# Split products that stream their moving operand, and write PSUM, from the last column to the first

## The chip, the cores and the metric

One core of one Trainium2 chip runs the whole program in one launch. The metric is the device time of that core in microseconds (us), from the median of several executions. The times of the engines come from one further execution that the hardware profiler recorded.

## The reference

512 tokens of width 1024 go through two blocks, all in float32. The first has two layers, each of them a half-weighted SwiGLU, a mixer (a bidirectional mLSTM in layer 0, a windowed attention in layer 1) and a second SwiGLU, with a layer norm after each. The second block has two layers of an HGRN2 mixer beside a sparse attention, and a SwiGLU, with RMS norms. Nearly all arithmetic lies in the projections `x @ w`:

```
def swiglu(x, w_in, w_out):
    gu = x @ w_in                      # 1024 -> 2 x 2816
    g, u = gu[..., :D_FF], gu[..., D_FF:]
    return (jax.nn.silu(g) * u) @ w_out
...
x = layer_norm(ALPHA * x + 0.5 * swiglu(x, ffn_w_in[l, 0], ffn_w_out[l, 0]), ...)   # six of these in all
...
p = x @ w_in                           # mLSTM, attention and the mixers of the second block
```

## The kernel before, in words

Activations lie with the features on the 128 partitions and the 512 tokens along the free axis, as eight tiles of 128x512. Every operand of a projection is split into two parts, a high part rounded to the type fp32r and the remainder (`split`, lines 171 to 177: ScalarE writes the high part, VectorE subtracts). A projection is then the sum of three products, high by high, high by low and low by high, accumulated in one PSUM bank. These are the split products. There are two places that issue them.

`mm3` (lines 202 to 208) takes a 128x128 block of the weights as the stationary operand and a token slice of the activations as the moving operand: all 512 tokens in `gemms` (kind "a") and in `out_head` and `out_early`, and a half of 256 tokens (HA, then HB) in `pre` and in `out_tail`. Its three products are lines 206, 207 and 208.

`gemms` (kind "b", lines 262 to 268) makes products whose result has tokens on the partitions. There a 128x128 block of the activations is stationary and the rows of the weights move, n = 512, 280 or 256 columns at a time. Its three products are lines 266, 267 and 268.

In both, each product has a weight load of its own. The order of the work on TensorE is written out by the program: generators are interleaved by estimated costs (`run`, `tick`), and each engine executes its instructions in that order. A semaphore makes a product wait for the split of its operands. Weights come by DMA from the SyncE queue, 512 KB at a time (line 183). Between two stages the norm of the last one is finished in two halves of 256 tokens, so that `pre` can start on the half HA while the half HB is still being normalised (lines 464 to 471 write x, xh and xl).

Other products on TensorE are not split products of these two places: plain float32 products (the mLSTM scores at line 687 and its values at line 716, line 1250 and more), transposes, and the attention scores at lines 880 and 1391. All the products' operands are contiguous along the free axis, except the moving operand of line 1250, which takes every second run of m columns, m = 1 to 64. Five small copies on VectorE read backwards: lines 619, 621, 643, 646 and 649 read rows 32 to 36 with a step of -1, right beside a forward twin (618, 620, 642, 645, 648).

Of the kernel before, what the change touches and what calls it, by code (L numbers as in the profile page):

```python
# [56 lines left out]
class Core:  # L57
# [128 lines left out]
    def weights(self, src, n=1024, at=None):  # L186
# [12 lines left out]
        self.v(n)  # L199
        return h, l  # L200

    def mm3(self, out, w, k, xh, xl, start, stop):
        mm = self.nc.tensor.matmul
        wh, wl = (a[k // 4][:, k % 4 * 128:k % 4 * 128 + 128] if isinstance(a, tuple) else a[:, k * 128:(k + 1) * 128]
                  for a in w)
        mm(out, wh, xh, start=start, stop=False)  # L206
        mm(out, wh, xl, start=False, stop=False)  # L207
        mm(out, wl, xh, start=False, stop=stop)  # L208
# [22 lines left out]
    def gemms(self, jobs):  # L231

        units = deque()
        for j in jobs:
            if j[0] == "a":
                units.append((j[1], 1024))
            else:
                units.extend((s, 2 * j[2]) for s in j[1])
        ready = deque()

        def nxt():
            while units and len(ready) < 2:
                ready.append(self.weights(*units.popleft()))
            return ready.popleft()
        for j in jobs:
            if j[0] == "a":
                w = nxt()
                p = self.bank()
                for k in range(KD):
                    self.mm3(p, w, k, self.xh[k], self.xl[k], k == 0, k == KD - 1)  # L250
                    yield 0.65
                j[2](p)
            else:
                n = j[2]
                if len(j) > 4:
                    yield j[4]
                ps = [self.bank() for _ in range(4)]
                mm = self.nc.tensor.matmul
                for kp in range(4):
                    h, l = nxt()  # L260
                    for i in range(2):
                        k = 2 * kp + i
                        wh, wl = h[:, i * n:(i + 1) * n], l[:, i * n:(i + 1) * n]
                        for t in range(4):
                            ts = slice(t * 128, (t + 1) * 128)
                            mm(ps[t][:, :n], self.xh[k][:, ts], wh, start=k == 0, stop=False)  # L266
                            mm(ps[t][:, :n], self.xh[k][:, ts], wl, start=False, stop=False)  # L267
                            mm(ps[t][:, :n], self.xl[k][:, ts], wh, start=False, stop=k == KD - 1)  # L268
                            yield 0.65 * n / 512
                j[3](ps)  # L270
# [1404 lines left out]
```

## Time and profile before

| | |
|---|---|
| time, median of 3 runs | 3350.8 us (3350.4 to 3352.97) |
| the profiled execution: its time, its span | 3350.13 us, 3348.3 us |
| TensorE busy (products) | 3305.9 us, 99% of the span, 18704 instructions |
| TensorE busy (weight loads, beside the products) | 2827.0 us, 84% |
| VectorE, ScalarE, GpSimd busy | 1686.3 us (50%), 1280.9 us (38%), 96.1 us (3%) |
| mean granted TensorE clock | 0.996 |
| moved by DMA | 304.04 MB, mean 91 GB/s |

The span is the time from the first to the last instruction; the profiled execution took 1.83 us more. A product's recorded duration is longer than its place in the queue: products are pipelined, so the rate is read from the distance between starts. "128*128 128x512" in a row is the stationary operand's shape and the result's partitions and columns.

### The profile page before, as it was taken

The numbers are of one execution on the slowest core, as the hardware profiler recorded it, in microseconds if no ns is written. First come the engines' busy times: TensorE is split into PE (matmuls) and PEld (weight loads), VectorE is DVE, ScalarE is ACT, GpSimd is POOL, SyncE is SP. The second block draws the span as 40 slices with busy tenths as digits, with TensorE's granted clock in tenths as the row PEclk, the third lists the DMA queues.
The fourth block names the chain that finished last, engine by engine and source line by source line (L and its number), as shares of the span: only waits on it lengthen the run. The fifth ranks groups of instructions, "written<-read, shape, count | busy, mean of one in ns | idle before, by whom it ended". The sixth has DMA issues, their size and how long they took to land.

```text
span 3348.3 us, 46248 instructions
## 1 busy us (share of the span) xinstructions
PE 3305.9 (99%) x18704; PEld 2827.0 (84%) x18704; DVE 1686.3 (50%) x3451; ACT 1280.9 (38%) x2231; POOL 96.1 (3%) x138
## 2 busy tenths in 40 slices
PE   8999999999999999999999989999999999999999
PEld 7888977988898888879888978788888988898888
DVE  4333756733354333787334667775333567853332
ACT  3322545522233222685222433563232335632221
POOL 0000011000000000110000000000000000000000
PEclk9999999999999999999999989999999999999999
DMA  4333322233332333212333523112333332023333
GB/s 143 96 94 97 100 76 64 89 97 98 93 109 89 100 94 108 74 41 89 95 98 98 163 88 94 45 51 82 99 95 94 107 115 64 26 72 102 98 101 95
DMA packets 88918, 304.04 MB, mean 91 GB/s; under 512 B 9857, under 2 KB 12417, under 8 KB 88705
## 3 DMA queue, kind: packets, MB, share of 16 engines
q1 hardware_dynamic: 88704, 301.10, 29.3%
q8 instruction: 146, 2.39, 0.3%
q14 instruction: 68, 0.55, 0.0%
HBM read 298.96 MB, written 2.10 MB: 90 GB/s over the span
## 4 chain that ended last, share of the span: by engine, by line
PE 94%; DVE 3%; ACT 2%; DMA 1%; issue 1%; POOL 0%; DVEq 0%; SPq 0%; ACTq 0%; POOLq 0%
PE b L206 26%; PE b L208 26%; PE b L207 26%; PE b L267 2%; PE b L268 2%; PE b L266 2%; PE b L1250 1%; PE b L1442 1%; PE b L1391 1%; PE b L1420 1%; PE b L716 1%; ACT wh L174 1%; DVE wl L177 1%; PE b L1303 1%; DMA wr<-w_in 1%
## 5 line engine op out<-in xcount | busy, mean ns | idle before, releaser
L174 ACT ACTIVATE wh<-wr 128x1024 fp32r<-128x1024 f32 (+3 forms) x532 | 545.0, 1026 | 1568.1 <-PE b L207 980.5
L177 DVE TENSOR_TENSOR wl<-wr,wh 128x1024 fp32r<-128x1024 f32 (+3 forms) x532 | 628.3, 1183 | 867.2 <-ACT wh L174 864.9
L206 PE MATMUL b<-xh,wh 128*128 128x512 f32 (+1 forms) x2712 | 1021.7, 378 | 9.5 <-ACT xh L174 7.4
L208 PE MATMUL b<-xh,wl 128*128 128x512 f32 (+1 forms) x2712 | 1008.8, 373 | 3.2 <-DVE wl L177 3.2
L207 PE MATMUL b<-xl,wh 128*128 128x512 f32 (+1 forms) x2712 | 1008.7, 373 | 2.9 <-DVE xl L177 1.8
L206 PEld LDWEIGHTS b<-xh,wh 128*128 128x128 f32 x2712 | 511.1, 189 | 105.5 <-issue 9.4
L208 PEld LDWEIGHTS b<-xh,wl 128*128 128x128 f32 x2712 | 512.5, 189 | 94.5 <-DVE wl L177 5.8
L207 PEld LDWEIGHTS b<-xl,wh 128*128 128x128 f32 x2712 | 513.1, 189 | 91.7 <-issue 3.5
L206 PE MATMUL b<-hh,wh 128*128 128x512 f32 (+1 forms) x1144 | 400.4, 350 | 0.0
L208 PE MATMUL b<-hh,wl 128*128 128x512 f32 (+1 forms) x1144 | 398.4, 348 | 0.0
L207 PE MATMUL b<-hl,wh 128*128 128x512 f32 (+1 forms) x1144 | 398.3, 348 | 0.0
L283 DVE SCALAR_TENSOR_TENSOR hf<-b,sg 128x512 f32<-128x512 f32 x132 | 90.7, 691 | 407.4 <-PE b L208 404.0
L206 PEld LDWEIGHTS b<-hh,wh 128*128 128x128 f32 x1144 | 216.5, 189 | 28.6 <-issue 1.0
L207 PEld LDWEIGHTS b<-hl,wh 128*128 128x128 f32 x1144 | 216.5, 189 | 28.5 <-issue 1.0
L208 PEld LDWEIGHTS b<-hh,wl 128*128 128x128 f32 x1144 | 216.5, 189 | 27.6
L267 PE MATMUL b<-wl,xh 128*128 128x512 f32 (+2 forms) x352 | 122.8, 349 | 4.3 <-DVE wl L177 4.2
L266 PE MATMUL b<-wh,xh 128*128 128x512 f32 (+2 forms) x352 | 125.1, 360 | 0.0
L268 PE MATMUL b<-wh,xl 128*128 128x512 f32 (+2 forms) x352 | 122.7, 349 | 0.0
L177 DVE TENSOR_TENSOR hl<-hf,hh 128x512 fp32r<-128x512 f32 x132 | 89.9, 685 | 0.0
L174 ACT ACTIVATE hh<-hf 128x512 fp32r<-128x512 f32 x132 | 82.8, 632 | 0.8
L1395 ACT ACTIVATE sc<-sc,nm 128x128 f32<-128x128 f32 (+3 forms) x128 | 71.1, 557 | 23.5 <-DVE nm L1393 22.5
L267 PEld LDWEIGHTS b<-wl,xh 128*128 128x128 f32 x352 | 67.2, 191 | 14.3 <-DVE wl L177 6.1
(408 smaller groups left out, 4122.1 us busy)
## 6 DMA issues: line engine op xcount, KB each, us to landing
wr<-w_in SPq DMA_DIRECT2D x176, 512.0 KB, 3.7
wr<-b_win SPq DMA_DIRECT2D x88, 512.0 KB, 3.7
wr<-w_out SPq DMA_DIRECT2D x80, 512.0 KB, 3.5
wr<-b_wout SPq DMA_DIRECT2D x36, 512.0 KB, 3.5
wr<-w_out SPq DMA_DIRECT2D x36, 384.0 KB, 3.1
wr<-b_out SPq DMA_DIRECT2D x20, 512.0 KB, 3.6
wr<-b_w SPq DMA_DIRECT2D x16, 512.0 KB, 3.8
wr<-b_wout SPq DMA_DIRECT2D x16, 384.0 KB, 3.2
```

Of the source, the lines that this page charges most:

```text
L174: nc.scalar.activation(h, src, AF.Copy)
L177: nc.vector.tensor_sub(l, src, h.bitcast(F32))
L206: mm(out, wh, xh, start=start, stop=False)
L207: mm(out, wh, xl, start=False, stop=False)
L208: mm(out, wl, xh, start=False, stop=stop)
L266: mm(ps[t][:, :n], self.xh[k][:, ts], wh, start=k == 0, stop=False)
L267: mm(ps[t][:, :n], self.xh[k][:, ts], wl, start=False, stop=False)
L268: mm(ps[t][:, :n], self.xl[k][:, ts], wh, start=False, stop=k == KD - 1)
L283: nc.vector.scalar_tensor_tensor(hf, pu, half, sg, op0=OP.mult, op1=OP.mult)
L716: nc.tensor.matmul(p[:, :257], w[:, (j - j0) * 128:(j - j0 + 1) * 128], v[s][:, h], start=s == ss[0], stop=s == ss[-1])
L1250: nc.tensor.matmul(p[:, i * 64:(i + 1) * 64], K[h][:, ts], q, start=True, stop=True)
L1395: nc.scalar.activation(sc[:, :N], sc[:, :N], AF.Exp, bias=nm[:, g:g + 1], scale=-1.0, accum_out=sm[:, g:g + 1])
```

## The change

A helper is added that reverses the free axis of the result and of the moving operand, and the two places that issue split products call it. The stationary operand is as before. As result and moving operand are reversed together, each result column ends up where it was.

```diff
+    def mm(self, out, w, x, start, stop):
+
+        self.nc.tensor.matmul(out[:, ::-1], w, x[:, ::-1], start=start, stop=stop)
+
     def mm3(self, out, w, k, xh, xl, start, stop):
-        mm = self.nc.tensor.matmul
+        mm = self.mm
...
                 ps = [self.bank() for _ in range(4)]
-                mm = self.nc.tensor.matmul
+                mm = self.mm
                 for kp in range(4):
```

The attention scores, the plain float32 products and the transposes call TensorE directly and stay as they are. No instruction is added, removed or moved, and no transfer changes.

## Rows read from the trace of the kernel before

**Rows 1.** The page's part 1: engine, busy us, share of the span, instructions.

```profile
PE 3305.9 (99%) x18704; PEld 2827.0 (84%) x18704; DVE 1686.3 (50%) x3451; ACT 1280.9 (38%) x2231; POOL 96.1 (3%) x138
```

**Rows 2.** The view of cores: span and mean granted clock.

```profile
core 0: 3348.3 us, clock 0.996
```

**Rows 3.** The page's part 4, the chain that ended last: by engine, by line.

```profile
PE 94%; DVE 3%; ACT 2%; DMA 1%; issue 1%; POOL 0%; DVEq 0%; SPq 0%; ACTq 0%; POOLq 0%
PE b L206 26%; PE b L208 26%; PE b L207 26%; PE b L267 2%; PE b L268 2%; PE b L266 2%; PE b L1250 1%; PE b L1442 1%; PE b L1391 1%; PE b L1420 1%; PE b L716 1%; ACT wh L174 1%; DVE wl L177 1%; PE b L1303 1%; DMA wr<-w_in 1%
```

**Rows 4.** PE waits: engine, line, what it waited for, us, times, longest.

```profile
PE b L206 <- ACT xh L174: 7.4, 2, 6.4
PE b L398 <- DVE lns L489: 6.2, 1, 6.2
PE b L267 <- DVE wl L177: 4.2, 2, 2.1
```

**Rows 5.** Groups by line and form, PE: count, busy us, mean ns, idle before.

```profile
L206 PE MATMUL b<-xh,wh 128*128 128x512 f32 x2248 | 891.6, 397 | 0.0
...
L206 PE MATMUL b<-hh,wh 128*128 128x512 f32 x704 | 273.9, 389 | 0.0
...
L266 PE MATMUL b<-wh,xh 128*128 128x512 f32 x192 | 75.8, 403 | 0.0
...
L266 PE MATMUL b<-wh,xh 128*128 128x256 f32 x96 | 28.9, 302 | 0.0
...
L266 PE MATMUL b<-wh,xh 128*128 128x280 f32 x64 | 20.3, 318 | 0.0
```

**Rows 6.** Line 206 by operand names: a mixed name, and the last of 16.

```profile
L206 PE MATMUL b<-q,wh x64: 277/283/682, 1493.2 to 1551.7; 128*128 128x256 f32 x48, 128*128 128x512 f32 x16
...
L206 PE MATMUL b<-xh,mh x16: 280/283/283, 378.8 to 402.1; 128*128 128x256 f32 x16
```

**Rows 7.** Timeline, 512 columns, first and last of 134: start, us, engine, line.

```profile
1199.63 0.39 PE L207 MATMUL b<-xl,wh 128*128 128x512 f32 x1
...
1229.78 0.39 PE L208 MATMUL b<-xh,wl 128*128 128x512 f32 x1
```

**Rows 8.** Timeline, 256 columns, first and last of 27: start, us, engine, line.

```profile
349.80 0.28 PE L208 MATMUL b<-hh,wl 128*128 128x256 f32 x1
...
352.92 0.28 PE L207 MATMUL b<-hl,xh 128*128 128x256 f32 x1
```

**Rows 9.** Timeline, plain float32 products (L687) between split products.

```profile
448.94 1.02 PE L687 MATMUL b<-qk,qk 128*128 128x512 f32 x2
449.40 0.80 PE L206 MATMUL b<-xh,wh 128*128 128x512 f32 x1
450.04 0.40 PE L207 MATMUL b<-xl,wh 128*128 128x512 f32 x1
```

**Rows 10.** Chain in order of time, plain float32 of 257 columns: start, us, count.

```profile
498.02 1.30 PE b L716 x6
```

**Rows 11.** Timeline of VectorE: forward copy and backward twin, 512 and 1280 elements.

```profile
404.25 0.41 DVE L618 COPY ig<-z 32x512 f32<-32x512 f32 x1
404.67 0.42 DVE L619 COPY ig<-z 4x512 f32<-4x512 f32 x1
...
419.52 0.81 DVE L642 COPY Un<-UU 32x1280 f32<-32x1280 f32 x1
420.34 0.82 DVE L643 COPY Un<-UU 4x1280 f32<-4x1280 f32 x1
```

**Rows 12.** Timeline, line 1250: runs of m=1 (first) and m=64 (last).

```profile
2040.74 1.00 PE L1250 MATMUL b<-Q,K 128*128 128x64 f32 x8
...
2077.76 1.00 PE L1250 MATMUL b<-Q,K 128*128 128x64 f32 x8
```

**Rows 13.** Groups by line and form, VectorE, norm between stages.

```profile
L465 DVE TENSOR_TENSOR x<-x,b 128x256 f32<-128x256 f32 x96 | 40.0, 416 | 0.9
```

## The prediction

> **What bounds the kernel now.** First the totals [rows 1]: TensorE's products are busy 99% of the span, VectorE 50%, ScalarE 38%. The clock was granted at 0.996 of full speed [rows 2], so TensorE sits at its upper level of 2.4 GHz nearly throughout. Then the chain that ended last [rows 3]: 94% of it is TensorE, and lines 206, 207 and 208 alone are 26% each. The waits confirm it [rows 4]: the longest sum that the products ever waited for is 7.4 us, and the whole idle time of TensorE is 3348.3 - 3305.9 = 42.4 us. The reader is to see that there is no other bound in this kernel. What a split product costs, the kernel costs, and nothing lies above it that could hide an added nanosecond.
>
> How many split products there are, and of what size: line 206 has 4,712 under 16 names. Of these 2,248 + 704 have 512 columns [rows 5], and 64 more stand in five mixed names (16 each for q, K and Qs, 8 each for qk and mh) [rows 6]: 3,016. The other 1,696 have 256 columns. Line 266 adds 192 of 512, 96 of 256 and 64 of 280 [rows 5]. Each stands for three products, so 3 x (3,016 + 192) = 9,624 of 512 columns, 3 x (1,696 + 96) = 5,376 of 256 and 3 x 64 = 192 of 280: 15,192 of the 18,704 products are touched.
>
> Their present price comes from the distance of starts, not from the recorded durations. Of 134 products of 512 columns in a row, first and last start 30.15 us apart [rows 7]: 30.15 / 133 = 226.7 ns each. Of 27 with 256 columns they start 3.12 us apart [rows 8]: 3.12 / 26 = 120 ns. The difference, 106.7 ns for 256 columns, is 0.417 ns a column, one column in each cycle of 2.4 GHz. What is left, 226.7 - 213.4 = 13.3 ns, belongs to the product and not to its columns; for 280 columns that makes 130 ns. So split products take 9,624 x 0.2267 + 5,376 x 0.120 + 192 x 0.130 = 2,182 + 645 + 25 = 2,852 us, 85% of the span.
>
> **The change part by part.** No instruction comes, goes or moves; queues, waits, weight loads and DMAs are the same. Each of 15,192 products gets a step of -1 in two places. The moving operand is read from SBUF downwards, and the result is written to PSUM downwards and, in all but the first of each accumulation, added to what is there. So the whole change is: 15,192 times (the price of a column read downwards and written downwards, less 0.417 ns, times the columns, plus whatever a downward start costs).
>
> The trace of before has no product with a negative step, so both sides are bounded by the nearest rows.
>
> The lower end, nothing. VectorE has copies that read float32 downwards, each beside a forward twin [rows 11]: 512 elements took 0.42 us against 0.41, and 1,280 took 0.82 against 0.81. From 512 to 1,280 the downward copy grows by 0.40 us for 768 elements, 0.52 ns an element, as the forward one does. A memory port that fed only rising addresses at this rate would show it here. TensorE's read wants 0.417 ns an element, not far above. For TensorE itself the only uneven moving read is line 1250: with every second element (m = 1) eight instructions take 1.00 us, and with runs of 64 (m = 64) also 1.00 us [rows 12]. That step is positive, and eight weight loads pace that stretch, so it only shows that such a read costs no more than the loads cover.
>
> The upper end, half the rate. If two neighbouring columns are taken together only in rising order, each column goes alone, at one in two of the present cycles. That rate has rows, the plain float32 products. Line 716 takes 1.30 / 6 = 0.217 us for 257 columns [rows 10], 0.843 ns a column. Of line 687 two products started at 448.94; the split product behind them is followed by its successor at 450.04 and so began about 0.227 us earlier, at 449.81 [rows 9]: 0.435 us for 512 columns. At these prices the change adds 9,624 x (0.435 - 0.2267) + 5,376 x (0.217 - 0.120) + 192 x (0.236 - 0.130) = 2,005 + 521 + 20 = 2,546 us. A gain has little room: below the column rate nothing can go, since one column a cycle is what the rows show at a full clock. Only the 13.3 ns a product could shrink.
>
> I take the lower end, nothing. The row nearest in kind, a downward float32 read next to its forward twin, shows no price at all. And nothing in the two operands' extents changes: each 512-column row is the same 2 KB, begun at its other end. This is a judgement on the read; for the write to PSUM no row of either direction tells anything, and that is where most of my doubt lies.
>
> Sum: 0 on the profiled execution's 3350.1 us (span 3348.3 us and 1.8 us around it), which stands 0.7 us under the median of the runs, 3350.8. Forecast: 3351 us.
>
> A rule that speaks against it: the Trainium skill, PSUM — Partial Sum Buffer, section "Specifications (TRN2)", gives PSUM lines of 8 bytes and says that "any non-contiguous AP slows matmuls significantly". Read to the letter, a step of -1 is not contiguous, and the sum would be that of the half rate. The Trainium skill, SBUF — State Buffer, section "Door 1: The DMA port swizzle", explains such penalties by lines: several consecutive accesses to the same line run at full bandwidth, each crossing to a new line costs. Two float32 columns next to each other share a line in either direction, and by that reading the sum is 0. The copies of [rows 11] agree with the second reading on VectorE's side; no row here shows a write to PSUM that would decide between them.
>
> **The rivals.**
>
> *Half rate (slower).* Place: the read of the moving row or the write to PSUM, in every split product; it decides as soon as either side handles one column where it now handles two. Price as above: 3350 + 2546 = about 5,900 us. With the columns at 0.843 ns and no fixed part it is 5,863, with the 13.3 ns kept on top of every product 6,068. Against it stand the downward copies [rows 11]; for it, that TensorE must move a column every 0.417 ns while the copy moves an element only every 0.52, and that the write has no witness. That the plain float32 products take twice as long per column [rows 10] shows only what such a rate would look like.
>
> *A fixed price per product (slower).* Each product already carries 13.3 ns beside its columns [rows 7, 8]. If a descending start doubles it, 15,192 x 13.3 ns = 202 us come on top: about 3,552 us. With no cover, it counts as slower from 6.7 / 15,192 us = 0.44 ns a product.
>
> *Waits that were not there (slower).* If the program's bookkeeping takes a reversed half row for the whole row, products on the half HA wait for the norm of HB. That norm is 8 blocks of three VectorE passes of about 0.416 us [rows 13], 10 us, at nine stage borders: at most 90 us, 3,440 us. Against it: the views are exact slices, only turned.
>
> *Far below half rate (slower).* If each column costs a full trip to memory, at four cycles a column, the 6.36 million columns add 6.36 x 3 x 0.417 = 7,950 us: about 11,300 us. No row comes near it.
>
> *A gain.* If the 13.3 ns of fixed time come from meeting the last result's end at the bank's upper edge, and vanish, up to 202 us go: 3,149 us. Nothing speaks for it; all products of a bank turn together, so the order of one behind the other is mirrored, not changed.
>
> *The change does nothing.* Turning both operands leaves the sum the same; if they are turned back on the way to the chip, the time stays too. In time this can't be told from the forecast.
>
> **How the numbers follow.** No change (the last rival included) 0.60, half rate 0.23, fixed price 0.08, new waits 0.02, far below half rate 0.04, a gain 0.03. A measurement of this kernel tells about 0.2%, 6.7 us, from no change. So faster 0.03, same 0.60, slower 0.37. The likeliest case by itself lies within 3344 to 3358 us. As only 0.60 lies there, the range for 8 in 10 must take in the half rate: from 3344 to 6070 us. It leaves out the gain and the case far below half rate, 0.07.
>
> **What the profile of the changed kernel would show.** If right: products of 512 columns start 227 ns apart and those of 256 start 120 ns apart, split products and untouched ones (lines 687, 716) alike; lines 206 to 208 keep about 26% of the chain each; TensorE's idle time stays near 42 us. Half rate shows as starts about 435 and 217 ns apart at an unchanged clock, with line 687 unchanged, and shares of VectorE and ScalarE falling by about 3350 / 5900. A fixed price shows as the same surplus at 512 and at 256 columns. New waits show as TensorE idle in front of line 206 for VectorE's xl or ScalarE's xh. The prediction is wrong if the starts move by more than half a nanosecond, or if a surplus grows with the columns.

## The result and the profile after

| | before | after |
|---|---|---|
| median (runs beside each other) | 3351.11 us (3350.4 to 3352.97) | 3405.93 us (3404.26 to 3407.57) |
| span of the profiled execution | 3348.3 us | 3403.6 us |

The ratio is 1.0163, with a 95% interval of 1.0145 to 1.018: the change makes the kernel slower by 54.8 us, 1.6%. The spans differ by 55.3 us.

Part 1 of the page, and the view of cores:

```profile
PE 3360.5 (99%) x18704; PEld 2825.6 (83%) x18704; DVE 1686.9 (50%) x3451; ACT 1281.5 (38%) x2231; POOL 95.1 (3%) x138
...
core 0: 3403.6 us, clock 0.995
```

Against [rows 1, 2]: the number of instructions is the same, the clock was granted at 0.995 against 0.996, VectorE and ScalarE are as busy as before, and TensorE's products have grown by 54.6 us. Its idle time is 3403.6 - 3360.5 = 43.1 us, against 42.4. So the time was not lost in waits; it lies inside the products. All six lines of split products now carry the helper's line, 204, with 82.7% of the chain; the six lines of before add up to as much, within the rounding of [rows 3].

Which products grew is read from the starts. Timeline of the changed kernel in the same stretch as [rows 7], 512 columns, first and last of 130 products; then 256 columns, first and last of 30, to be held against [rows 8]:

```profile
1199.84 0.40 PE L204 MATMUL b<-xh,wl 128*128 128x512 f32 x1
...
1229.94 0.40 PE L204 MATMUL b<-xh,wl 128*128 128x512 f32 x1
...
351.40 0.28 PE L204 MATMUL b<-hh,wh 128*128 128x256 f32 x1
...
354.83 0.28 PE L204 MATMUL b<-hh,wl 128*128 128x256 f32 x1
```

512 columns: 30.10 us / 129 = 233.3 ns a product, 6.7 ns more than 226.7. 256 columns: 3.43 us / 29 = 118.3 ns, 1.7 ns less than 120. With the counts of the prediction: 9,624 x 6.67 - 5,376 x 1.7 = 64.2 - 9.1 = 55.1 us, against 55.3 us between the spans (the 192 products of 280 columns are left out). That is closer than the runs repeat: those of the changed kernel alone lie up to 3.3 us apart. The plain float32 products, which the change does not touch, keep their pace (line 716 is now 720; from the chain in order of time, to be held against [rows 10]):

```profile
475.02 1.30 PE b L720 x6
```

So the surplus belongs neither to the product (256 columns would show it) nor evenly to its columns (256 would show half of it).

### The profile page after: what moved, and what is told of

It is laid out like the page before. It is cut to its first block, busy times and chain, and to the rows that moved or that the text cites. A ratio compares the mean times of both kernels' runs of the same rounds, so it can differ in the third digit from the quotient of the medians.

```text
span 3403.6 us, 46267 instructions
## 1 busy us (share of the span) xinstructions
PE 3360.5 (99%) x18704; PEld 2825.6 (83%) x18704; DVE 1686.9 (50%) x3451; ACT 1281.5 (38%) x2231; POOL 95.1 (3%) x138
## 4 chain that ended last, share of the span: by engine, by line
PE 94%; DVE 2%; ACT 1%; DMA 1%; issue 1%; POOL 0%; DVEq 0%; SPq 0%; ACTq 0%; POOLq 0%
PE b L204 83%; PE b L1254 1%; PE b L1446 1%; PE b L1395 1%; PE b L1424 1%; PE b L720 1%; DMA wr<-w_in 1%; PE b L935 1%; PE b L1307 1%; DVE wl L177 1%; ACT wh L174 1%; PE b L915 1%; PE b L884 0%; PE b L409 0%; PE b L691 0%
## 5 line engine op out<-in xcount | busy, mean ns | idle before, releaser
L204 PE MATMUL b<-xh,wh 128*128 128x512 f32 (+1 forms) x2712 | 1039.8, 385 | 9.5 <-ACT xh L174 7.5
L204 PE MATMUL b<-xh,wl 128*128 128x512 f32 (+1 forms) x2712 | 1027.1, 379 | 3.2 <-DVE wl L177 3.1
L204 PE MATMUL b<-xl,wh 128*128 128x512 f32 (+1 forms) x2712 | 1026.5, 379 | 3.1 <-DVE xl L177 2.0
L204 PEld LDWEIGHTS b<-xh,wh 128*128 128x128 f32 x2712 | 511.0, 189 | 118.4 <-issue 9.4
L174 ACT ACTIVATE hh<-hf 128x512 fp32r<-128x512 f32 x132 | 82.7, 631 | 0.8
```

The costliest lines, as they stand in the source:

```text
L174: nc.scalar.activation(h, src, AF.Copy)
L204: self.nc.tensor.matmul(out[:, ::-1], w, x[:, ::-1], start=start, stop=stop)
```

## The experiments

Two theories at first: READ, the downward read of the moving operand costs it, and WRITE, the downward write to PSUM does. Each time is held against runs of the kernel before on the same chip.

**Read alone, write alone.** The helper's one line becomes, in the two kernels:

```diff
-        self.nc.tensor.matmul(out[:, ::-1], w, x[:, ::-1], start=start, stop=stop)
+        self.nc.tensor.matmul(out, w, x[:, ::-1], start=start, stop=stop)     # k_read
+        self.nc.tensor.matmul(out[:, ::-1], w, x, start=start, stop=stop)     # k_write
```

> All split products read downwards but write upwards, so each result row is mirrored (the values are not those of the reference). READ: the whole surplus stays, 3406 us. WRITE: 3351 us. If the two sides share it: in between.

> All split products write downwards but read upwards (the values are not those of the reference). READ: 3351 us. WRITE: 3406 us. If the surplus needs both sides: 3351 us in this run and in the one that reads downwards alone.

Measured: reading downwards alone 3402.27 us, ratio 1.0154 (1.0138 to 1.0169); writing downwards alone 3352.75 us, ratio 1.0007 (0.9998 to 1.0016). READ holds, WRITE is refuted. The timelines in the stretch from 1200 us say the same, first and last of 130 products when reading downwards, then of 134 when writing downwards:

```profile
1199.79 0.40 PE L204 MATMUL b<-xl,wh 128*128 128x512 f32 x1
...
1229.89 0.40 PE L204 MATMUL b<-xl,wh 128*128 128x512 f32 x1
```

```profile
1199.63 0.39 PE L204 MATMUL b<-xh,wh 128*128 128x512 f32 x1
...
1229.78 0.39 PE L204 MATMUL b<-xl,wh 128*128 128x512 f32 x1
```

30.10 / 129 = 233.3 ns and 30.15 / 133 = 226.7 ns.

**Only the products of 256 columns.**

```diff
+        if x.shape[-1] == 256:
+            out, x = out[:, ::-1], x[:, ::-1]
+        self.nc.tensor.matmul(out, w, x, start=start, stop=stop)
```

> Only the products of 256 columns are reversed on both sides, those of 512 and 280 are as before. If the surplus belongs to 512 columns alone, as the starts in the changed kernel's trace have it, nothing is added: 3351 us, or by 5376 x (118.8 - 120) ns = -6 us about 3345 us. A fixed price per product of 3.6 ns (54.8 us over 15,192 products) would give 3351 + 5376 x 3.6 ns = 3370 us.

Measured: 3343.6 us beside 3350.24, ratio 0.9979 (0.997 to 0.9988). No price at 256 columns, rather the small gain that their starts showed. The timeline of this kernel, 256 columns, first and last of 28, 3.19 / 27 = 118.1 ns:

```profile
349.76 0.28 PE L206 MATMUL b<-hh,wh 128*128 128x256 f32 x1
...
352.95 0.28 PE L206 MATMUL b<-hh,xh 128*128 128x256 f32 x1
```

This version is 0.2% faster than the kernel before, and so faster than the changed one too.

**The forms by themselves.** Each stretch is 96 products in a row that differ in one thing; the pace is read from the starts. The core of it, here for 512 columns read downwards and written upwards:

```diff
+        for j in range(96):
+            o, ww, xx, s, e = args(j, 512)     # wh*xh, wh*xl, wl*xh in turn, 24 to a bank
+            nc.tensor.matmul(o, ww, xx[:, ::-1], start=s, stop=e)
```

> This kernel does none of the reference's work: it runs stretches of 96 products in a row on fixed operands, each with a weight load of its own, and times one form per stretch. In the changed kernel 512 columns went from 226.7 to 233.3 ns a product (+6.6) and 256 columns from 120 to about 119. Theory READ: the downward read of the moving operand costs it, so at 512 columns read-reversed alone gives 233 and write-reversed alone 227. Theory WRITE: the other way round, 227 and 233. Over the sizes 512, 448, 384, 320, 256, both reversed against both forward: a fixed price per product gives +6.6 ns at 512, 448, 384 and 320; a price per column (0.013 ns) gives +6.6, +5.8, +5.0, +4.1; either must explain why 256 shows none. If the surplus lies in adding to what is in PSUM, it is gone where every product starts anew. Plain float32, already at half the column rate, and bf16: READ through the bytes per cycle gives no surplus for both, WRITE gives a surplus of about 6 ns for bf16 too.

The rows of five stretches, by line: 512 columns read and written up and up (57), down and down (62), down and up (67), up and down (72), and 320 columns down and down (122). A row has the first of each three products; its first and last start are 93 products apart.

```profile
L57 PE MATMUL b<-xh,wh x32: 389/389/389, 29.6 to 50.7; 128*128 128x512 f32 x32
...
L62 PE MATMUL b<-xh,wh x32: 397/397/398, 51.4 to 73.1; 128*128 128x512 f32 x32
...
L67 PE MATMUL b<-xh,wh x32: 397/397/398, 73.8 to 95.5; 128*128 128x512 f32 x32
...
L72 PE MATMUL b<-xh,wh x32: 389/389/402, 96.2 to 117.3; 128*128 128x512 f32 x32
...
L122 PE MATMUL b<-xh,wh x32: 311/311/312, 278.1 to 291.7; 128*128 128x320 f32 x32
```

21.1 us where the read rises (21.1 / 93 = 227 ns), 21.7 us where it falls (233 ns), whatever the write does. Over the sizes (from the starts, to a hundredth of a us, in steady running):

| columns | 512 | 448 | 384 | 320 | 256 |
|---|---|---|---|---|---|
| read upwards, ns | 226.7 | 202.7 | 173.3 | 146.7 | 120.0 |
| read downwards, ns | 233.3 | 206.6 | 177.8 | 146.7 | 118.4 |

Surplus +6.7, +3.9, +4.5, 0 and -1.6 ns: neither of the two laws that were offered. At 512 columns the pair stays 226.7 and 233.3 also where every product starts anew instead of adding, and where each goes to the next bank. So neither the direction of the write, nor the adding, nor the bank has a part in it. Plain float32 takes 429.2 ns and bf16 216 ns in both directions. Neither shows a surplus, as READ had expected. The bf16 row does not run into the 13.3 ns either that the upward split products carry (16 ns at 448 columns): 216 - 213.3 = 2.7 ns.

**What in the read.** MEET and START stood against ORDER.

> This kernel does none of the reference's work: stretches of 96 products of the split type, all written upwards, that differ in how the moving operand is read, in the stationary operand's columns, or in where the moving row begins. Theory MEET: the surplus comes from the weight load that runs beside the product (the plain float32 and bf16 products of the first such kernel showed 0 between the two directions). Then with a stationary operand of 64 or 32 columns both the 13.3 ns above the column rate of the forward product and the 6.7 ns between the directions shrink or go, and beginning the moving row elsewhere in its tile may shift them. Theory START: a downward read costs 6.7 ns where it begins; then it stays at 64 and 32 stationary columns, and a row read as two halves, each downwards, costs it twice, 240 ns against 233. Theory ORDER: it hangs on the order inside a group of four columns or on the order of the groups: one of the two rows that turn only one of them has 233, the other 227. Two halves swapped but each read upwards: 227 under START and ORDER. Forward and backward rows in turn: 230 under START, and under MEET anything.

Rows of this kernel, all 512 columns: stationary operand of 32 columns, read up (85) and down (90); halves in order, each downwards (150); groups of 4 downwards but upwards inside (160), groups of 4 upwards but downwards inside (165); every second column, upwards (170); a row that begins at column 4 of its tile, upwards (185).

```profile
L85 PE MATMUL b<-yh,wh x32: 390/394/402, 119.7 to 141.2; 128*32 128x512 f32 x32
...
L90 PE MATMUL b<-yh,wh x32: 395/395/398, 141.9 to 163.6; 128*32 128x512 f32 x32
...
L150 PE MATMUL b<-yh,wh x32: 394/397/398, 321.1 to 342.8; 128*128 128x512 f32 x32
...
L160 PE MATMUL b<-yh,wh x32: 396/397/398, 365.3 to 387.0; 128*128 128x512 f32 x32
...
L165 PE MATMUL b<-yh,wh x32: 389/389/402, 387.7 to 408.8; 128*128 128x512 f32 x32
...
L170 PE MATMUL b<-yh,wh x32: 615/630/637, 409.4 to 451.6; 128*128 128x512 f32 x32
...
L185 PE MATMUL b<-yh,wh x32: 388/392/402, 498.0 to 519.5; 128*128 128x512 f32 x32
```

ORDER holds for single rows: with the groups turned a product takes 21.7 us / 93 = 233 ns, with only their insides turned 21.1 / 93 = 227 ns. START falls: two downward halves cost no more than one downward row (233 ns). MEET falls in the form it had: with 32 stationary columns the downward read keeps its 233 ns, and the upward one gets slower, 231 to 232 ns, so the gap between the two nearly closes from the other side. At 256 columns it is otherwise, and there the 13.3 ns shrink as MEET had it: with 64 and with 32 stationary columns the upward read takes 113.3 ns and the downward one 117.8, so that the downward read, ahead at the full width, falls behind. Loading the same stationary block each time changes nothing (226.7 and 233.3 ns). An upward read that begins at column 2, 4, 8 or 16 of its tile loses too, 229 to 233 ns; beginning at 64 or 256 it has 226.7. The good pace is thus the special one, and it hangs on where in its tile the row begins.

Forward and backward rows in turn gave 233.3, not the 230 of START. ORDER does not give it either: if each product paid for its own order alone, the mean would be 230. So a product's pace hangs on its neighbours too, and how is not shown. And every second column took 42.2 / 93 = 454 ns: half the rate, which no row of a split product had shown before.

**How large is the unit.** LINE or BLOCK.

> This kernel does none of the reference's work: stretches of 96 products of the split type, written upwards, that differ in the order in which the moving columns are read. The run before it had 233.3 ns a product with groups of 4 columns (16 bytes) downwards and 226.7 ns with the elements turned inside such groups alone. Theory LINE: what counts is that successive groups of 4 columns fall; then groups of 2 (which also fall inside the 4) and of 4 have 233, while groups of 8 to 128 columns downwards, which mostly rise, come back to 227. Theory BLOCK: a larger unit counts; the pace stays at 233 up to some size of group and is 227 beyond it, since the two halves swapped had 226.7. At 256 columns: 118.4 where 512 columns have 233, 120 where they have 227. Groups from the two halves in turn rise in each half and jump between: 227 under LINE only if jumps upwards and back cancel, more if every change of block costs.

Rows, 512 columns: groups of 8 (80), 32 (90) and 64 (95) downwards, upwards inside; groups of 16 (105) and 64 (110) upwards, downwards inside:

```profile
L80 PE MATMUL b<-yh,wh x32: 395/396/398, 96.4 to 118.1; 128*128 128x512 f32 x32
...
L90 PE MATMUL b<-yh,wh x32: 390/393/404, 141.2 to 162.8; 128*128 128x512 f32 x32
...
L95 PE MATMUL b<-yh,wh x32: 389/389/393, 163.5 to 184.6; 128*128 128x512 f32 x32
...
L105 PE MATMUL b<-yh,wh x32: 427/432/433, 207.0 to 231.8; 128*128 128x512 f32 x32
...
L110 PE MATMUL b<-yh,wh x32: 397/397/403, 232.6 to 254.3; 128*128 128x512 f32 x32
```

Groups of 2, 4, 8 and 16 columns downwards keep 233 ns, 32 has 232.4, and 64 and 128 are back at 226.7. At 512 columns BLOCK holds, with a unit of 64 columns, which are 256 bytes. The begin of a row ceased to matter between column 16 and 64; 32 was not run. The order of such blocks is free; a falling order inside them is not (beyond groups of 4, line 165), and it costs the same 6.7 ns when the blocks themselves rise (line 110). A broken order costs more than a falling one: groups of 16 that rise, each read downwards, take 24.8 / 93 = 267 ns, and groups of 4 and 16 from the two halves in turn take 250 and 240 ns; groups of 64 in turn are back at 227. LINE's 227 failed for groups of 8, 16 and 32.

At 256 columns the expectation failed in part. Groups of 2 downwards took 118.4 ns, and groups of 64 and 128 took 120, as expected; but groups of 8 took 120.0, of 16 117.8 and of 32 118.7, where 118.4 was expected. Groups of 16 rising, each read downwards, took 133 ns. So the unit of 64 columns is shown for products of 512 columns.

**The same at full size.** The split products read and write groups of 4 columns, once with the groups turned, once with their insides:

```diff
+        out, x = (a.rearrange("p (g c) -> p g c", c=4)[:, ::-1] for a in (out, x))        # k_lines
+        out, x = (a.rearrange("p (g c) -> p g c", c=4)[:, :, ::-1] for a in (out, x))     # k_inner
```

> All split products read and write groups of 4 columns from the last to the first, upwards inside each group; the sums are those of the reference. LINE or BLOCK: as the changed kernel, 3406 us, or the 3402 us of the kernel that only read downwards. If the order inside the groups costs: 3351 us.

> All split products read and write groups of 4 columns in rising order, downwards inside each group; the sums are those of the reference. LINE or BLOCK: 3351 us, as before the change. If the order inside the groups costs: 3406 us.

Measured: 3404.18 us, ratio 1.0157 (1.014 to 1.0174), and 3350.02 us, ratio 0.9999 (0.9989 to 1.0008). The second has a step of -1 in both operands of every split product and costs nothing that these runs can tell.

## Why the prediction was right or wrong

The time lies in the range, 3344 to 6070 us, but that says little for the mechanism: the range was that wide to take in the half rate. The likeliest case, no change, did not come. Slower had a chance of 0.37, most of it for the half rate; the case nearest to what came, the fixed price, had 0.08. The prediction's own sign of being wrong was there: the starts moved by 6.7 ns, more than half a nanosecond.

- *What bounds the kernel* was right, and it carries the result: nothing hid the added nanoseconds, and 6.7 ns times 9,624 products went into the time, less what 256 columns gave back.
- *The counts and the paces* were right. With the measured paces put in, the sum gives 55.1 of 55.3 us.
- *"I take the lower end, nothing"* is the step that failed, and with it the row it leaned on. VectorE's copies [rows 11] showed that a step of -1 is all but free for VectorE's read (0.42 us against 0.41). TensorE's read of a split product is another: at 512 columns it took 233.3 ns downwards against 226.7 upwards, by the order inside blocks of 64 columns. The copies were the nearest row in kind, but they are reads of another engine; and the second of them, line 643, falls only inside runs of 128 elements. The doubt stood in the wrong place as well: *"for the write to PSUM no row of either direction tells anything, and that is where most of my doubt lies"*. The write is free (ratio 1.0007); the read pays.
- *The fixed price per product* came nearest, with its sign and the threshold of 0.44 ns a product, and was wrong as a law: it was to show at 512 and at 256 columns alike, and its size was 13.3 ns. Measured are 6.7 ns at 512 columns and -1.6 ns at 256.
- *Half rate* is refuted for a step of -1. The rate itself exists: every second column took 454 ns.
- *New waits* are refuted: TensorE's idle time changed by 0.7 us. *The change does nothing* and *far below half rate* are refuted by the starts. *A gain* by the 13.3 ns did not come; 256 columns gave back 1.6 ns of them.
- Two sums of the half rate are off by a few us: from the rates given, 5,863 and 6,068 come to about 5,860 and 6,060. Nothing hangs on it.
- The sentence of the Trainium skill, PSUM — Partial Sum Buffer, section "Specifications (TRN2)", that any access pattern which is not contiguous slows products significantly has no support here for a step of -1: writing downwards left 226.7 ns as it was. Of the Trainium skill, SBUF — State Buffer, section "Door 1: The DMA port swizzle", one half agrees: order inside 16 bytes is free (line 165, 227 ns). The other does not. Every second float32 still falls twice into each line of 16 bytes, which that section has at full bandwidth, and it ran at half rate (454 ns); and order over more than a line costs, up to 256 bytes.

Open is why. What is shown is that only the read counts, that at 512 columns the unit is 64 columns (if it goes by columns or by 256 bytes is not shown), that the surplus of 512, 448, 384, 320 and 256 columns is +6.7, +3.9, +4.5, 0 and -1.6 ns, and that it appears in the products of fp32r and not in plain float32 or bf16. That a row's pace also shifts with its begin and with the number of stationary columns would fit two readers that get in each other's way. The second would be the weight load, which runs beside every product. Its records, here for 512 columns read upwards (65) and for every second column (170), give a hint:

```profile
L65 PEld LDWEIGHTS b<-yh,wh x32: 187/188/188, 30.8 to 51.9; 128*128 128x128 f32 x32
...
L170 PEld LDWEIGHTS b<-yh,wh x32: 188/207/208, 409.2 to 451.1; 128*128 128x128 f32 x32
```

The same load took 207 ns instead of 188 beside the uneven read. But it took 188 ns beside the downward read too, and no run leaves the load out, so this cause is not shown.

## What to carry to other kernels

Where one engine is busy 99% of the span, a few nanoseconds an instruction are the whole effect; read the pace from the distance of starts over a hundred instructions, for each size apart, since a mean over 512 and 256 columns would have hidden that one lost and the other gained. A row of another engine is a weak witness, even if the operation looks the same; a stretch of 96 products in the form asked for settles it. Keep the moving rows of fp32r products of 512 columns rising inside each 64 columns, and begin them where the good pace was measured, at column 0, 64 or 256 of the tile.

## What the runs showed of the hardware that was not expected

- Split products of 512 columns took 226.7 ns a product where the moving row begins at column 0, 64 or 256 of its tile, at the full stationary width. Beginning at column 2, 4, 8 or 16 they took 233.3, 231.6, 233.3 and 228.9 ns.
- Fewer stationary columns do not make a product of 512 columns faster: 226.7 ns with 128, 230.0 with 64, 231.7 with 32. At 256 columns, read upwards, they do: 120, 113.3 and 113.3 ns.
- At 256 columns and the full stationary width a downward read is faster than an upward one, 118.4 against 120 ns, and that is worth 0.2% of this kernel. With 64 or 32 stationary columns it is slower, 117.8 against 113.3 ns.
